# Doubling keys and queries into the other 64 partitions: a DMA in place of a GpSimd copy

## The chip, the cores and the metric

The kernel runs on one core of a Trainium2 chip. The metric is device time in microseconds from one launch; times stand as the median of the timed runs. The engines are TensorE (matrix products), VectorE, ScalarE, GpSimd and SyncE (SP in the profile), which issues DMAs; the DMAs themselves run on 16 DMA engines.

## The reference

One inference step of a two-layer encoder for 512 prompt frames and 32 sample frames (the sample has a past of 1024 frames). Each layer projects the normed input, runs three kinds of attention, gates and merges them, and then runs a feed-forward layer with a short convolution. The three kinds are stick-breaking attention (SB, 8 heads of 64), differential attention (DF, 4 heads with two maps of 64) and latent attention (ML, 8 heads). Cut to what the change touches:

```python
def sb_block(q, q_pos, k, v, k_pos):
    z = jnp.einsum('bqhd,bkhd->bhqk', q, k).astype(jnp.float32) * SB_SCALE
    ...
def diff_block(q, q_pos, k, v, k_pos, lam):
    s = jnp.einsum('bqhmd,bkhmd->bhmqk', q, k).astype(jnp.float32) * DIFF_SCALE
    ...
dq = rmsnorm(z_dq.reshape(B, S, DIFF_HEADS, 2, DIFF_DIM), w['diff_qn_g'])
```

All of it is in float32. The kernel gets this accuracy out of TensorE's rounded format by writing each operand as a high part (rounded) and a low part (the rest).

## The kernel before

The activations lie transposed: 128 features on the partitions, 544 frames (32 sample, 512 prompt) along them. A layer has twelve attention units of 128 features: SB 0 to 3, DF 0 to 3, ML 0 to 3. For an SB or DF unit, `qkv_tasks` (L731) projects keys, then values, then queries, each with 48 matmuls of 272 columns (8 slices, 3 products of parts, 2 halves); between them come projections of gates, which fill TensorE.

A score contracts over 64 features only, half of the partitions. So that one matmul can take high and low part at once, one operand is stacked (`to_stack`, L653: tile u, high parts in one half of the partitions and low parts in the other) and the other doubled (`to_dbl`, L676: tile kk, each head's high and low part present in both halves). SB doubles the keys and stacks the queries; DF doubles the queries and stacks the keys. `to_dbl` therefore runs 16 times: four SB key tiles and four DF query tiles in each of two layers. For each head h, `copy` (ScalarE) writes the rounded high part of 64x512, `tt` (VectorE) the low part of 64x512, and `rnd(..., "pool")` (GpSimd, `pscale`) copies both, 64x1024, into the other half of the partitions. Then the 32 sample frames are split into kn, a part of the same tile. There are two buffers of kk.

The readers are `sb_chain` (L1012) and `df_score` (L1228), which need the doubled tile under the name "k" or "q", and `sb_sample` (L902) and `df_sample` (L1137), which need kn under "kn" or "qn".

The order of the instructions on every engine is not written by hand. `Sched` (L114) simulates the kernel while it is built: every chain of work is a generator (a fiber) with a time at which it is next ready, the one that is ready first is stepped, and each operation adds its estimated duration to its engine (`op`, L127) and 125 ns to the fiber. `put` (L188) files a result with the time at which it is due, `need` (L191) holds a reader until then. The engines then run the resulting lists strictly in order, with semaphores.

All weights come in through SP's queue: `loader` (L214) issues 512 KB loads into four buffers ws, in order of the plan, each when a buffer comes free; the splits into parts (ScalarE, then VectorE, tile wx) free them. Stores of results and the loads of the DF distance tables (alp, als) go through the same queue.

Of the kernel before, what the change touches and what calls it, by code (L numbers as in the profile page):

```python
# [9 lines left out]
F32 = mybir.dt.float32  # L10
# [300 lines left out]
class Kern:  # L311
# [364 lines left out]
    def to_dbl(self, dst, name, z):  # L676


        t = yield from self.al(self.A, [128, 2176], "kk", F32R)
        kk = t[:, :2048].rearrange("p (h s c) -> p h s c", h=2, s=2)  # L680
        kn = t[:, 2048:2112].rearrange("p (s c) -> p s c", s=2)
        rs = (slice(0, 64), slice(64, 128))
        for h, r in enumerate(rs):
            self.copy(kk[r, h, 0], z[r, TS:])
            yield
            self.tt(kk[r, h, 1], z[r, TS:], kk[r, h, 0].bitcast(F32), ALU.subtract)
            yield
            self.rnd(kk[rs[1 - h], h], kk[r, h].bitcast(F32), "pool")
            yield
        yield from self.split(kn, z[:, :TS])  # L690
        self.s.put(dst, name, kk)
        self.s.put(dst, name + "n", kn)

    def zeroed(self, shape, tag):
        t = yield from self.al(self.A, shape, tag, F32R)
# [1807 lines left out]
```

## Time and profile before

| | us |
|---|---|
| median of 3 timed runs | 2085.48 (2082.34 to 2085.56) |
| the profiled execution's own time | 2083.75 |
| its span, first to last instruction | 2082.1 |
| TensorE busy | 2030.7 (98%) |
| VectorE busy | 1614.9 (78%) |
| ScalarE busy | 1310.2 (63%) |
| GpSimd busy | 492.2 (24%) |

In the rows below, PE is TensorE, DVE VectorE, ACT ScalarE, POOL GpSimd and SPq the queue of SyncE. A group of instructions is written as line, engine, operation, tile written <- tiles read, shape. "<-" inside brackets or at the end of a row names what ended the engine's wait. Buffer numbers are left out of the names, so kk stands for both buffers.

### The profile page before, as it was taken

How to read it: one execution, taken by the hardware profiler on the slowest of the kernel's cores; microseconds unless marked ns; L12 is line 12 of the kernel's file. 1: busy time of each engine (PE TensorE's matmuls, PEld its weight loads, DVE VectorE, ACT ScalarE, POOL GpSimd, SP SyncE). 2: the span in 40 equal slices, each digit the busy share in tenths (PEclk: the TensorE clock that was granted, in tenths of full speed). 3: DMA queues.
4: the chain of work that ended last, by engine and by line, in shares of the span. 5: the costliest groups of instructions: out<-in, count | busy, mean ns of one | idle time of the engine just before them, and what ended most of it. 6: DMA issues, size and time to landing. Idle time of an engine off the chain costs nothing.

```text
span 2082.1 us, 42033 instructions
## 1 busy us (share of the span) xinstructions
PE 2030.7 (98%) x15926; PEld 1984.5 (95%) x15926; DVE 1614.9 (78%) x3419; ACT 1310.2 (63%) x2889; POOL 492.2 (24%) x810
## 2 busy tenths in 40 slices
PE   7999999999999999999999999999999999999999
PEld 7999999988999999999989999999889999999999
DVE  7897887888685996598568878887886869955973
ACT  6887676877554564366468777667775555644651
POOL 1344322334200221032023343313342002210310
PEclk9999999999999999999999999999999999999999
DMA  5333433421663232332433334333216622323332
GB/s 205 103 104 125 137 125 107 129 73 48 207 200 111 73 101 84 110 99 86 130 121 104 104 125 149 120 107 112 80 41 219 206 93 91 92 83 102 102 90 87
DMA packets 86218, 238.45 MB, mean 115 GB/s; under 512 B 10304, under 2 KB 11200, under 8 KB 86016
## 3 DMA queue, kind: packets, MB, share of 16 engines
q1 hardware_dynamic: 82240, 223.51, 33.7%
q0 software_dynamic: 3776, 12.26, 1.7%
q8 instruction: 125, 2.05, 0.4%
q14 instruction: 77, 0.63, 0.1%
HBM read 201.52 MB, written 34.21 MB: 113 GB/s over the span
## 4 chain that ended last, share of the span: by engine, by line
PE 77%; DVE 12%; ACT 4%; issue 4%; DMA 1%; POOL 1%; SPq 0%; POOLq 0%; ACTq 0%; DVEq 0%
PE z L410 41%; PE g L410 26%; PE pv L410 8%; DVE wx L347 2%; PE z L416 2%; DVE tf L347 1%; DVE w L347 1%; ACT w L340 1%; ACT p L340 1%; DVE tr L347 1%; DMA ws<-wts 1%; ACT wx L340 1%; DVE pk L347 1%; DVE kk L347 1%; DVE sgl L355 1%
## 5 line engine op out<-in xcount | busy, mean ns | idle before, releaser
L410 PE MATMUL g<-h,wx 128*128 128x272 f32 x5208 | 761.1, 292 | 9.2 <-ACT wx L340 9.0
L410 PEld LDWEIGHTS g<-h,wx 128*128 128x128 f32 x5208 | 696.7, 189 | 17.4 <-ACT wx L340 9.0
L410 PE MATMUL z<-act,wx 128*128 128x272 f32 x4632 | 586.7, 288 | 5.6 <-DVE wx L347 5.6
L410 PEld LDWEIGHTS z<-act,wx 128*128 128x128 f32 x4632 | 581.6, 189 | 6.7 <-DVE wx L347 6.7
L340 ACT ACTIVATE wx<-ws 128x512 fp32r<-128x512 f32 (+2 forms) x554 | 306.9, 555 | 392.9 <-PE z L410 256.3
L347 DVE TENSOR_TENSOR wx<-ws,wx 128x512 fp32r<-128x512 f32 (+2 forms) x554 | 338.6, 612 | 205.9 <-ACT wx L340 202.1
L410 PE MATMUL z<-h,wx 128*128 128x272 f32 x1368 | 179.0, 289 | 0.0
L410 PEld LDWEIGHTS z<-h,wx 128*128 128x128 f32 x1368 | 174.8, 190 | 0.0
L340 ACT ACTIVATE w<-z 128x256 f32<-128x256 f32 (+9 forms) x212 | 91.6, 441 | 44.9 <-PE pv L410 26.2
L347 DVE TENSOR_TENSOR tf<-g,rstd 128x272 f32<-128x272 f32 x184 | 80.0, 435 | 39.8 <-PE g L410 34.7
L2054 POOL COPY conv<-ap 128x2 f32<-128x2 f32 x34 | 21.1, 622 | 317.2 <-DVE ap L347 317.2
L1917 POOL COPY conv<-ap 128x2 f32<-128x2 f32 x10 | 18.2, 1816 | 300.0 <-DVE ap L347 300.0
L410 PE MATMUL pv<-w,vst 128*128 128x512 f32 (+3 forms) x352 | 81.8, 322 | 3.2 <-DVE w L347 1.8
L2041 POOL COPY ap<-gp 128x2 f32<-128x2 f32 x34 | 63.8, 1876 | 81.0 <-ACT wx L340 59.7
L340 ACT ACTIVATE wy<-ws 128x512 fp32r<-128x512 f32 x68 | 42.9, 631 | 60.2 <-PE z L410 34.9
L368 POOL TENSOR_SCALAR tr<-tf 128x544 fp32r<-128x544 f32 (+2 forms) x66 | 45.8, 693 | 141.1 <-ACT tf L340 97.7
L355 DVE SCALAR_TENSOR_TENSOR cc<-ap,gp,cc 128x546 f32<-128x546 f32 x88 | 68.8, 782 | 4.0 <-ACT cc L340 3.8
L340 ACT ACTIVATE p<-p 128x512 f32<-128x512 f32 (+4 forms) x160 | 70.2, 463 | 1.1
L340 ACT ACTIVATE wx<-sgl 128x512 fp32r<-128x512 f32 x102 | 63.4, 627 | 11.1 <-PE z L410 7.1
L347 DVE TENSOR_TENSOR wx<-sgl,wx 128x512 fp32r<-128x512 f32 x102 | 67.7, 685 | 2.3 <-ACT wx L340 2.2
L368 POOL TENSOR_SCALAR kk<-kk 64x1024 fp32r<-64x1024 f32 x32 | 40.6, 1268 | 119.8 <-DVE kk L347 108.4
L347 DVE TENSOR_TENSOR w<-z,w 128x512 fp32r<-128x512 f32 (+5 forms) x124 | 55.9, 466 | 16.3 <-ACT w L340 16.1
(273 smaller groups left out, 3676.4 us busy)
## 6 DMA issues: line engine op xcount, KB each, us to landing
ws<-wts SPq DMA_DIRECT2D x246, 512.0 KB, 3.6
ws<-wts SPq DMA_DIRECT2D x56, 256.0 KB, 3.0
ws<-wts SPq DMA_DIRECT2D x36, 384.0 KB, 3.0
sgl<-sig SPq DMA_DIRECT2D x46, 272.0 KB, 3.2
ws<-wts SPq DMA_DIRECT2D x32, 320.0 KB, 3.0
sig<-tf SPq DMA_DIRECT2D x36, 272.0 KB, 2.1
tf<-od POOLq DMA_DIRECT2D x24, 272.0 KB, 4.7
od<-oa SPq DMA_DIRECT2D x16, 272.0 KB, 2.5
```

Of the source, the lines that this page charges most:

```text
L340: self.nc.scalar.activation(out=out, in_=in_, func=func, **kw)
L347: self.nc.vector.tensor_tensor(out=out, in0=in0, in1=in1, op=op)
L355: self.nc.vector.scalar_tensor_tensor(out=out, in0=in0, scalar=scalar, in1=in1, op0=op0, op1=op1)
L368: self.nc.gpsimd.tensor_scalar(out=out, in0=in_, scalar1=s1, scalar2=1.0, op0=ALU.mult, op1=ALU.mult)
L410: self.nc.tensor.matmul(out=out, lhsT=lhsT, rhs=rhs, start=start, stop=stop, skip_group_check=not chk)
L416: self.nc.tensor.transpose(out, in_, self.ident[:p, :p])
L1917: nc.gpsimd.tensor_copy(out=cv[:, 0:2], in_=ap[:, 546:548])
L2041: nc.gpsimd.tensor_copy(out=ap[:, 0:2], in_=self.gain(G_ST + 2 * i, 2))
L2054: nc.gpsimd.tensor_copy(out=cv[:, 0:2], in_=ap[:, 546:548])
```

## The change

In `to_dbl`, the two GpSimd copies of a tile become two DMAs on SP's queue. The planner is told nothing of an engine for them; instead the doubled tile is due 2500 ns after the second DMA is issued, and kn is filed first, with its own time.

```diff
-            self.rnd(kk[rs[1 - h], h], kk[r, h].bitcast(F32), "pool")
+            self.nc.sync.dma_start(out=kk[rs[1 - h], h].bitcast(F32), in_=kk[r, h].bitcast(F32))
+            late = self.s.cur.ready + 2500.0
             yield
         yield from self.split(kn, z[:, :TS])
+        self.s.put(dst, name + "n", kn)
+        self.s.cur.ready = max(self.s.cur.ready, late)
         self.s.put(dst, name, kk)
-        self.s.put(dst, name + "n", kn)
```

## Rows read from the trace of the kernel before

**Rows 1.** The page's totals: busy us, share of the span, instructions.
```profile
PE 2030.7 (98%) x15926; PEld 1984.5 (95%) x15926; DVE 1614.9 (78%) x3419; ACT 1310.2 (63%) x2889; POOL 492.2 (24%) x810
```
**Rows 2.** Windows by stage: window, its length, busy us of PE, PEld, DVE, ACT, POOL.
```profile
40.00:370.00 330.00, 327.41 (x2583) 315.12 (x2582) 272.65 (x640) 244.94 (x584) 112.34 (x212) 1.00 0.36 120
370.00:545.00 175.00, 165.88 (x1246) 157.16 (x1245) 141.60 (x315) 127.31 (x321) 62.46 (x89) 0.99 0.27 84
1080.00:1405.00 325.00, 321.92 (x2541) 309.46 (x2540) 265.89 (x627) 238.98 (x566) 109.86 (x209) 1.00 0.35 116
1405.00:1580.00 175.00, 165.71 (x1232) 156.81 (x1231) 140.29 (x312) 125.66 (x318) 61.80 (x89) 0.98 0.26 84
```
**Rows 3.** Waits of PE: who ended them, us in total, times, longest us.
```profile
PE z L416 <- POOL p L368: 2.6, 7, 0.6
...
PE z L410 <- DVE w L347: 2.2, 2, 1.1
```
**Rows 4.** Tile kk's own view: ns of one, least, median and most; first and last start.
```profile
L347 DVE TENSOR_TENSOR kk<-tf,kk x48: 171/676/1012, 31.5 to 1370.0; 64x512 fp32r<-64x512 f32 x32, 128x32 fp32r<-128x32 f32 x16
```
**Rows 5.** Groups by shape: busy us, mean ns of one, idle before.
```profile
L368 POOL TENSOR_SCALAR kk<-kk 64x1024 fp32r<-64x1024 f32 x32 | 40.6, 1268 | 119.8 <-DVE kk L347 108.4 <-DVE w L347 11.0
...
L347 DVE TENSOR_TENSOR tr<-tf,tr 128x544 fp32r<-128x544 f32 x46 | 33.0, 718 | 4.9 <-POOL tr L368 4.5
...
L347 DVE TENSOR_TENSOR w<-w,w 128x544 fp32r<-128x544 f32 x8 | 7.1, 883 | 0.0
```
**Rows 6.** Timeline of unit DF1 in layer 0: start us, us, engine, line, operation.
```profile
254.51 1.71 SPq L219 DMA_DIRECT2D ws<-wts  x3
...
255.73 1.01 DVE L347 TENSOR_TENSOR kk<-tf,kk 64x512 fp32r<-64x512 f32 x1
...
256.89 1.04 POOL L368 TENSOR_SCALAR kk<-kk 64x1024 fp32r<-64x1024 f32 x1 [0.69 <-DVE kk L347]
...
257.13 1.38 DVE L347 TENSOR_TENSOR w<-w,w 128x544 fp32r<-128x544 f32 x1
...
258.57 0.51 PE L410 MATMUL z<-w,cr 128*128 128x512 f32 x2 [1.09 <-DVE w L347]
...
260.14 0.56 PE L410 MATMUL z<-u,kk 128*128 128x128 f32 x4
```
**Rows 7.** DMA issues: queue, count, KB each, median us from issue to landing.
```profile
dk<-tf SPq DMA_DIRECT2D x8, 272.0 KB, 2.1
...
b<-als SPq DMA_DIRECT2D x8, 264.0 KB, 5.0
b<-alp SPq DMA_DIRECT2D x8, 256.0 KB, 4.2
```
**Rows 8.** Timelines of SB0, DF0, DF2, DF3, layer 0: second subtraction, first reader.
```profile
37.05 0.69 DVE L347 TENSOR_TENSOR kk<-tf,kk 64x512 fp32r<-64x512 f32 x1
...
40.88 1.51 PE L410 MATMUL z<-u,kk 128*128 128x128 f32 x8
...
218.95 0.81 DVE L347 TENSOR_TENSOR kk<-tf,kk 64x512 fp32r<-64x512 f32 x1
...
224.20 0.97 PE L410 MATMUL z<-u,kk 128*128 128x128 f32 x7
...
292.71 0.69 DVE L347 TENSOR_TENSOR kk<-tf,kk 64x512 fp32r<-64x512 f32 x1
...
295.66 1.08 PE L410 MATMUL z<-u,kk 128*128 128x128 f32 x8
...
329.75 0.69 DVE L347 TENSOR_TENSOR kk<-tf,kk 64x512 fp32r<-64x512 f32 x1
...
334.45 0.73 PE L410 MATMUL z<-u,kk 128*128 128x128 f32 x5
```
**Rows 9.** Timeline of ScalarE: a wait for a weight load in layer 0.
```profile
231.68 0.63 ACT L340 ACTIVATE wx<-ws 128x512 fp32r<-128x512 f32 x1 [2.01 <-DMA ws<-wts]
```
**Rows 10.** Windows, columns as in rows 2: 225 to 245 us.
```profile
225.00:245.00 20.00, 19.89 (x148) 18.61 (x147) 18.37 (x58) 14.03 (x36) 7.34 (x11) 1.00 0.50 162
```

## The prediction

> **What bounds the kernel now.** I read the page's totals first. TensorE is busy 98% of the span, GpSimd 24% [rows 1]: the engine from which work is taken is far from being the bound, and the engine that is the bound keeps all its instructions. A gain can therefore only come out of TensorE's idle time. Second I read the windows by stage, because a share over the whole span says nothing of the stage that is edited. The doubling belongs to the stick-breaking and differential units, which run in 40 to 370 us (layer 0) and 1080 to 1405 us (layer 1). There TensorE is idle 330.00 - 327.41 = 2.59 us and 325.00 - 321.92 = 3.08 us, together 5.67 us; the latent-attention stages behind them, which double nothing with this helper, are idle 9.12 and 9.29 us, 18.41 us in all [rows 2]. So if the edit removed every wait in its own stages it would win 5.67 us, 0.27% of the time. Third come the waits of TensorE: GpSimd ends only 2.6 us of them, and these are on the probability tile p, not on kk; two waits of 1.1 us each end with VectorE on the tile w [rows 3]. No row there names kk.
>
> **What the edit removes.** 32 GpSimd copies of 64x1024, mean 1268 ns: two for each of 16 doubled tiles (eight SB key tiles, eight DF query tiles), 40.6 us of GpSimd [rows 5]. GpSimd is not late for TensorE on kk, so those 40.6 us as such are worth nothing. What they cost is what they do to VectorE. The subtraction that makes the low half of kk takes 676 ns in the median and 1012 ns at most [rows 4]; the subtraction on w of 128x544 takes 883 ns in the mean, where the same shape on tr takes 718 [rows 5]. The timeline of unit DF1 shows why that matters: VectorE's kk subtraction of 1.01 us, then a GpSimd copy of kk at 256.89, and across it the w subtraction, 1.38 us from 257.13; TensorE then waits 1.09 us for exactly that w [rows 6]. Without the copies the two subtractions should take about 0.68 and 0.72, so VectorE gives back 0.33 + 0.66 = 1.0 us ahead of that wait. The wait occurs twice, once in each layer, 2.2 us in total [rows 3]. I book **-2.2 us** (bounds: 0, if another subtraction is late next; -5.7, if all idle time of the two stages went).
>
> [...]
>
> **What the edit adds on the DMA side.** 32 transfers of 64 partitions x 4096 bytes, 256 KB, from SBUF to SBUF on SP's queue, 8.4 MB beside the 238 MB that are moved already. The trace has no SBUF-to-SBUF transfer and none between partition halves. Nearest rows, issue to landing: 2.1 us for the store dk<-tf of 272 KB from 128 partitions; 4.2 us for the 256 KB load alp; 5.0 us for the 264 KB load als, the only large one on 64 partitions, which always goes out right behind alp [rows 7]. So 2.1 is the end below, with a free queue, and 5.0 the end above, behind other traffic. I take 2.1 where no weight load was issued within the microsecond ahead, and 4.2 where the transfer falls into a train of them.
>
> [...]
>
> What hides the transfer is the room between the end of a tile's second subtraction and the first matmul that reads the tile. For the SB keys it is wide: keys are projected first, and the V and Q projections stand between, 96 matmuls at 330/2583 = 128 ns [rows 2], over 12 us; only the first unit of layer 0 is tight, 37.74 to 40.88 = 3.1 us [rows 8], still above 2.1. For the DF queries, which are projected last, the room is 224.20 - 219.76 = 4.44 us (DF0), 260.14 - 256.74 = 3.40 (DF1) [rows 6, 8], 295.66 - 293.40 = 2.26 (DF2) and 334.45 - 330.44 = 4.01 (DF3) [rows 8]; layer 1 repeats them to within a few tenths. Set against these: DF0 2.1 in 4.44, nothing; DF1 falls behind the train of three weight loads that SP issues from 254.51 on [rows 6], 4.2 - 3.40 = 0.8 us; DF2 2.1 in 2.26, which the issue and the semaphores use up, 0.3 us; DF3 2.1 in 4.01, nothing. TensorE takes its instructions in order, so such a wait is paid in full. 1.1 us a layer, **+2.2 us** (bounds: 0, and with 5.0 everywhere the 11.8 us of the rival below).
>
> **SP's queue.** The transfer waits on SP for VectorE's subtraction, and behind it stand weight loads, the loads of past keys and values, alp and als, and the stores. At some 0.33 us an issue SP's own time is 32 x 0.33 = 10.6 us of a mostly waiting engine. The cover is the lead of the weights. The trace has a natural test: ScalarE sat idle 2.01 us, up to 231.68, until a weight load landed, and TensorE was nevertheless busy 19.89 of the 20.00 us from 225 to 245 [rows 9, 10]. Some two microseconds of delay on this queue thus cost nothing. If that cover were gone, each microsecond would be paid once for each of the 16 tiles. I book 0.
>
> **The planner.** The order of all engines is written out by a simulation (Sched), and the edit changes its inputs. Before, kk was due after the second subtraction plus copy, plus both parts of kn: 125 + 1254 + 125 + 122 + 125 + 108 + 125 = 1984 ns by the kernel's own formulas. After it is due 125 + 2500 = 2625 ns behind that subtraction, but the subtraction itself comes 1254 + 125 = 1379 ns earlier, as the first half's copy no longer stands ahead of it: 2625 - 1984 - 1379 = 738 ns earlier in all. The small tile kn, which the sample path reads, is due about 2.8 us earlier, as both copies are gone ahead of it. Both move order in the edited stages. The TensorE idle of the two layers is 9.12 and 9.29 us in the stage behind, although the layers come in differently [rows 2], so the plan falls back into the same order after a disturbance, and I book 0 with a few microseconds either way.
>
> **Sum.** -2.2 + 2.2 + 0 + 0 = 0. The profiled execution took 2083.75 us (2082.1 of span and 1.65 around it), 1.73 below the median 2085.48 of the three timed runs. The four executions average 2084.3, and that is the forecast: no change.
>
> **Rivals.**
> 1. *The transfers are late for TensorE* (slower). Price: each of the eight DF tiles takes 5.0 us. Then 0.56 + 1.60 + 2.74 + 0.99 = 5.9 us a layer, 11.8 in all, less 2.2 gained: 2084.3 + 9.6 = 2093.9 us. It decides from a landing of about 2.3 us on in DF2 and 3.4 us in DF1. For it: the als row, the weight train at 254.51, and that the planner allows only 2.5 us. Against it: stores on a free queue land in 2.1 us, and three of the four units leave 3.4 us or more. Chance 0.25.
> 2. *VectorE's relief shortens more than the two w waits* (faster), and the earlier kn lets the units end earlier, so that the latent stage meets more gate projections to fill its 18.4 us of idle. Price: the 5.7 us of the edited stages gone, or a third of the 18.4 with the w waits: 2084.3 - 5.7 = 2078.6, or 2084.3 - 6.1 - 2.2 = 2076.0. For it: VectorE is the second busiest engine, 272.65 of 330 us [rows 2]. Against it: TensorE is already 99.2% busy there, and the idle latent stage waits for chains in which kk has no part. Chance 0.18.
> 3. *It does not matter at all*: transfers hidden, the w wait taken over by the next late subtraction; also about 2084. It is within the forecast's band.
>
> **How the numbers follow.** A change of 0.2%, 4.2 us, is about what a measurement of this kernel can tell from none. The forecast and rival 3 hold 0.57, with a band of their own of 2081 to 2088. Rival 1 beyond 4.2 us holds 0.25, rival 2 beyond 4.2 us 0.18. The range reaches most of the way to both: 2078.5 below (rival 2 by the edited stages alone), 2092 above (three quarters of rival 1).
>
> **What would show it.** In the profile after: GpSimd near 492 - 41 = 452 us; a row kk<-kk among the DMA issues, 32 of 256 KB, its landing time the judge between forecast (2 to 3 us) and rival 1 (4 to 5); the waits of TensorE with or without a row that ends in that DMA; the 1.1 us waits on w gone and the VectorE mean on w near 720 ns; the idle time of the windows 40 to 370 and 1080 to 1405 near 2.5 us each. The forecast is wrong if TensorE waits over 6 us for kk transfers, or if idle time outside the two stages moves by more than 4 us.

## The result, and the profile after

| | before | after |
|---|---|---|
| median of 5 runs each, us | 2082.66 (2081.20 to 2085.56) | 2094.67 (2091.87 to 2097.63) |
| ratio after / before, 95% interval | | 1.0052 [1.0041, 1.0062] |
| span of the profiled execution, us | 2082.1 | 2092.9 |
| TensorE idle: span less busy, us | 51.4 | 58.5 |

The runs before are the three timed ones and two more. The changed kernel is 0.52% slower, about 12 us. The forecast of no change was wrong, and the time lies above its range.

The totals of the page after (busy us, share of the span, instructions), to be read beside [rows 1]:

```profile
PE 2034.4 (97%) x15926; PEld 1987.6 (95%) x15926; DVE 1608.4 (77%) x3419; ACT 1305.9 (62%) x2889; POOL 450.8 (22%) x778
```

The edit did what it says: GpSimd lost 32 instructions and 41.4 us. The same TensorE instructions now take 3.7 us more of busy time and have 7.1 us more of idle time between them: 10.8, the difference of the two spans.

The windows by stage after (the columns of [rows 2]: window, length, busy us of PE, PEld, DVE, ACT, POOL, granted clock, DMA share, GB/s). The edges are moved with the stages. The five short windows belong to the paragraph on the clock below:

```profile
40.00:377.00 337.00, 331.30 (x2590) 317.66 (x2590) 270.92 (x640) 244.21 (x587) 91.72 (x198) 0.99 0.41 128
377.00:552.00 175.00, 165.93 (x1249) 157.47 (x1248) 140.76 (x314) 126.39 (x320) 64.26 (x89) 0.99 0.26 85
1088.00:1415.00 327.00, 320.45 (x2512) 308.91 (x2512) 261.19 (x621) 234.96 (x562) 88.56 (x193) 0.99 0.39 124
1415.00:1590.00 175.00, 165.19 (x1246) 155.86 (x1245) 141.46 (x314) 126.54 (x319) 64.01 (x89) 1.00 0.27 86
296.00:300.00 4.00, 2.00 (x14) 1.70 (x14) 2.24 (x8) 1.57 (x4) 0.64 (x1) 0.94 0.79 242
300.00:305.00 5.00, 5.00 (x31) 5.00 (x31) 3.32 (x12) 2.94 (x10) 0.56 (x2) 0.70 0.28 79
...
1295.00:1300.00 5.00, 1.43 (x13) 1.32 (x11) 2.94 (x7) 1.80 (x4) 1.07 (x2) 0.97 1.00 274
1300.00:1305.00 5.00, 5.00 (x30) 5.00 (x31) 2.03 (x8) 1.57 (x5) 0.00 (x0) 0.69 0.23 91
...
1340.00:1345.00 5.00, 5.00 (x30) 5.00 (x30) 3.44 (x13) 2.51 (x10) 0.03 (x1) 0.66 0.36 121
```

The time came in where the edit is. TensorE idles 337.00 - 331.30 = 5.70 us in the edited stage of layer 0 and 6.55 in that of layer 1, where [rows 2] had 2.59 and 3.08. The latent-attention stages idle 9.07 and 9.81, as in [rows 2] (9.12 and 9.29).

The waits of TensorE after (who ended them, us in total, times, longest), beside [rows 3]:

```profile
PE z L410 <- DMA kk<-kk: 11.3, 11, 3.6
...
PE z L416 <- POOL p L368: 2.6, 7, 0.6
...
PE z L410 <- DVE w L347: 0.5, 1, 0.5
```

A new row heads the list. Eleven waits, 11.3 us, end with the new transfers; the two waits of 1.1 us on w are gone, as forecast, and one of 0.5 us stands at another place. The row of the transfers among the DMA issues after (queue, count, KB each, median us from issue to landing):

```profile
kk<-kk SPq DMA_DIRECT2D x32, 256.0 KB, 4.0
```

The planner allows them 2.5 us and the forecast took 2.1 for most. They take 4.0 in the median, and from 2.8 to 5.8.

The timeline of two units after, DF2 in layer 0 and DF1 in layer 1 (start us, us, engine, line, operation; in brackets the wait ahead of it and who ended it):

```profile
291.60 1.39 DVE L347 TENSOR_TENSOR kk<-tf,kk 64x512 fp32r<-64x512 f32 x2
291.61 0.33 SPq L219 DMA_DIRECT2D ws<-wts  x1
292.33 1.15 SPq L688 DMA_DIRECT2D kk<-kk  x2
...
297.95 0.41 PE L410 MATMUL z<-u,kk 128*128 128x128 f32 x2 [1.59 <-DMA kk<-kk]
...
298.76 0.94 PE L410 MATMUL z<-u,kk 128*128 128x128 f32 x6 [0.41 <-DMA kk<-kk]
...
1292.49 0.47 SPq L688 DMA_DIRECT2D kk<-kk  x1
1293.06 0.52 SPq L219 DMA_DIRECT2D ws<-wts  x1
...
1293.93 0.47 SPq L688 DMA_DIRECT2D kk<-kk  x1
...
1299.88 1.41 PE L410 MATMUL z<-u,kk 128*128 128x128 f32 x5 [3.57 <-DMA kk<-kk]
```

In DF2 both subtractions now run back to back, both transfers go out together 0.7 us behind a 512 KB weight load (ws), and they land 5.5 and 5.6 us after their issue. In DF1 of layer 1 a weight load comes between the two: the first transfer lands in 2.9 us and the second in 5.8, and TensorE waits 3.57 us, the longest of the eleven. Read so over all 32 transfers, the ten that go out less than a microsecond behind a weight load land in 4.1 to 5.8 us, the eight that go out while no weight load is in flight in 2.8 to 3.8, and the fourteen with an earlier load still in flight in 2.9 to 5.6.

**The clock behind the waits.** After the waits of DF2 the granted clock from 300 to 305 us is 0.70, and TensorE gets through 31 matmuls; behind the 3.57 us wait it is 0.69, and behind DF2 of layer 1, which waited 1.53 and 0.32 us at 1338 to 1340, it is 0.66. Part of each stretch ran at 0.50: read by single microseconds, the granted clock is 0.50, 0.50, 0.52, 1.00 and 1.00 from 300 on, 0.50, 0.50, 0.50, 0.96 and 1.00 from 1300 on, and 0.81, 0.50, 0.50, 0.50 and 0.98 from 1340 on. Before, the stretch of 300 to 305 us held 36 matmuls at 1.00, and no 5 us stretch of the two edited stages lay below 0.90. By the granted clock the three stretches lost 5 x (0.30 + 0.31 + 0.34) = 4.75 us, an estimate; TensorE's busy time rose by 3.7.

A fall of the clock does not follow every such wait. The kernel with due 5500 (below) was profiled twice. At about 700 us, outside the edited stages, TensorE waits 1.97 us in one profile and 2.00 in the other; the 5 us that follow, in this order:

```profile
700.70:705.70 5.00, 5.00 (x30) 5.00 (x29) 5.00 (x12) 3.34 (x5) 2.74 (x1) 0.67 0.34 108
...
698.70:703.70 5.00, 5.00 (x40) 5.00 (x41) 5.00 (x11) 3.03 (x5) 2.25 (x1) 1.00 0.36 108
```

Their busy times differ by 4.0 us (2030.6 and 2026.6), so the 3.7 of one pair of profiles measures little. Over the timed runs the mean granted clock is 0.993 in the changed kernel (five runs, 0.992 to 0.994) and 0.996 in the kernel before (the 23 runs beside the first four experiments, 0.994 to 0.998): 0.003 of 2090 us, some 6 us, an estimate. But the kernel with only the queries by DMA (below), which is as slow, has 0.996 as well. What the clock cost the change as a whole stays open.

### The profile page after: what moved, and what is told of

It reads as the page before. It is cut to its first block, busy times and chain, and to the rows that moved or that the text cites. A ratio compares the mean times of both kernels' runs of the same rounds, so it can differ in the third digit from the quotient of the medians.

```text
span 2092.9 us, 42063 instructions
## 1 busy us (share of the span) xinstructions
PE 2034.4 (97%) x15926; PEld 1987.6 (95%) x15926; DVE 1608.4 (77%) x3419; ACT 1305.9 (62%) x2889; POOL 450.8 (22%) x778
## 4 chain that ended last, share of the span: by engine, by line
PE 78%; DVE 11%; ACT 4%; issue 4%; DMA 2%; POOL 1%; SPq 0%; ACTq 0%; POOLq 0%; DVEq 0%
PE z L410 41%; PE g L410 27%; PE pv L410 8%; PE z L416 2%; DVE wx L347 2%; DMA kk<-kk 2%; DVE tf L347 1%; ACT p L340 1%; ACT w L340 1%; ACT wx L340 1%; DVE kk L347 1%; DVE tr L347 1%; DVE nm L372 1%; ACT tf L340 1%; DVE sgl L355 1%
## 5 line engine op out<-in xcount | busy, mean ns | idle before, releaser
L368 POOL TENSOR_SCALAR tr<-tf 128x544 fp32r<-128x544 f32 (+2 forms) x66 | 50.3, 762 | 160.0 <-ACT tf L340 117.7
L410 PE MATMUL z<-u,kk 128*128 128x384 f32 (+3 forms) x256 | 54.2, 328 | 11.5 <-DMA kk<-kk 11.3
```

The lines of the kernel that those rows point to most:

```text
L368: self.nc.gpsimd.tensor_scalar(out=out, in0=in_, scalar1=s1, scalar2=1.0, op0=ALU.mult, op1=ALU.mult)
L410: self.nc.tensor.matmul(out=out, lhsT=lhsT, rhs=rhs, start=start, stop=stop, skip_group_check=not chk)
```

## The experiments

Theory A: the time is lost because the transfers of the DF query tiles land later than the first reader asks for them. Its rivals: the new plan (kn filed first, another due time) costs the time by itself; or the transfers are fast, and it is SP's queue, where they stand behind weight loads, that makes them late. "Stage" below is the time from the first z<-u,kk matmul of a layer to its first z<-kk,u matmul, both layers added: the SB and DF units and the projections that the plan puts between them and behind them. (The number of its matmuls differs by a dozen from plan to plan, some 1.5 us at 128 ns each; kernels with the same plan have the same number.) It is 731.8 us before and 740.2 after. The kernel that ran twice (5500, below) gives 724.7 and 724.1, which shows how well it repeats.

**Keys by DMA, queries by GpSimd.**

```diff
-            self.nc.sync.dma_start(out=kk[rs[1 - h], h].bitcast(F32), in_=kk[r, h].bitcast(F32))
-            late = self.s.cur.ready + 2500.0
+            late = 0.0
+            if name == "k":
+                self.nc.sync.dma_start(out=kk[rs[1 - h], h].bitcast(F32), in_=kk[r, h].bitcast(F32))
+                late = self.s.cur.ready + 2500.0
+            else:
+                self.rnd(kk[rs[1 - h], h], kk[r, h].bitcast(F32), "pool")
```

> The DMA for the 8 SB key tiles alone; the 8 DF query tiles are copied by GpSimd as before. Theory A: no wait of TensorE for kk transfers, as V and Q projections stand between; 2081 to 2085 us. Theory B: in between, about 2088. Theory C: half of the loss, about 2088.

Measured 2079.30 us, ratio 0.9980 [0.9972, 0.9989]: faster than before, and below the range of each theory. No wait of TensorE ends with a transfer. The keys' transfers are hidden, and taking GpSimd off the SB units, with the plan that goes with it, is worth some 4 us.

**Queries by DMA, keys by GpSimd.** The same edit with `if name == "q"`.

> The DMA for the 8 DF query tiles alone; the 8 SB key tiles are copied by GpSimd as before. Theory A: the full loss, about 11 us of waits for kk transfers, 2092 to 2096 us. Theory C: half of the loss, about 2088.

Measured 2094.59 us, ratio 1.0053 [1.0041, 1.0066], the whole of the loss. The wait of TensorE in its profile:

```profile
PE z L410 <- DMA kk<-kk: 9.1, 13, 1.4
```

The loss hangs on the eight DF query tiles, as theory A has it. Its waits are 2.2 us fewer than after and its time is the same, so it probably lacks what the keys' half brings.

**The new plan with the old copies.** The GpSimd copy stands where the DMA stood, and the planner is told nothing of it; the order of TensorE's instructions is that of the changed kernel.

```diff
-            self.nc.sync.dma_start(out=kk[rs[1 - h], h].bitcast(F32), in_=kk[r, h].bitcast(F32))
+            self.nc.gpsimd.tensor_scalar(out=kk[rs[1 - h], h], in0=kk[r, h].bitcast(F32), scalar1=1.0, scalar2=1.0,
+                                         op0=ALU.mult, op1=ALU.mult)
```

> The planner is told exactly what it is told in the changed kernel (no GpSimd time, due 2500 ns later, kn filed first), but the copies still run on GpSimd. Theory A: no loss, 2081 to 2085 us, as the copy is done 1.1 to 1.3 us after the subtraction, inside 2.5. Theory B: the loss is there without a single transfer, about 2093 us.

Measured 2085.45 us, ratio 1.0006 [0.9997, 1.0015]. The plan by itself costs nothing that can be told, so that rival falls. It also parts the order from the copies in the waits on w. With the copies still there the w subtraction of 128x544 takes 714 ns in the mean, where [rows 5] had 883: the new order moved it from under the copy, and the two waits in DF1 are gone. But two others, of 0.83 and 1.31 us, have come among the SB units of layer 1, and the sum is nearly that of [rows 3]:

```profile
PE z L410 <- DVE w L347: 2.1, 2, 1.3
```

In the same order without the copies, the changed kernel has 0.5 us of such waits. So the order moved the waits on w, and the copies' absence took 1.6 us of them away.

**The transfer with a later due time.** The only edit is that the planner takes 5.5 us for a transfer.

```diff
-            late = self.s.cur.ready + 2500.0
+            late = self.s.cur.ready + 5500.0
```

> Same transfers as the changed kernel; only the time at which the planner takes a doubled tile to be due goes from 2500 to 5500 ns after the issue. Theory A (TensorE waits because the query tiles land 4.4 to 5.8 us after their issue while the readers are ordered for 2.5): the 11.3 us of waits for kk transfers fall under 2 us, the time comes back to 2081 to 2085 us. Theory B (the new order costs by itself): another order again, no forecast, nearer 2095. Theory C (the 8.4 MB of added traffic and the issues on SP's queue cost): unchanged, 2093 to 2096.

Measured 2077.39 us, ratio 0.9969 [0.9958, 0.9981]: faster than both kernels, and below the range of theory A. Its totals (busy us, share, instructions):

```profile
PE 2030.6 (98%) x15926; PEld 1986.3 (96%) x15926; DVE 1609.3 (77%) x3419; ACT 1308.5 (63%) x2889; POOL 448.1 (22%) x778
```

Its waits of TensorE on w and kk (us in total, times, longest):

```profile
PE z L410 <- DVE w L347: 0.9, 2, 0.4
PE z L410 <- DMA kk<-kk: 0.4, 1, 0.4
```

Its timeline of DF2 in layer 0:

```profile
288.22 0.33 SPq L219 DMA_DIRECT2D ws<-wts  x1
...
291.65 1.60 SPq L688 DMA_DIRECT2D kk<-kk  x2
...
298.35 1.09 PE L410 MATMUL z<-u,kk 128*128 128x128 f32 x8
```

The same bytes go through the same queue in as many transfers; what is gone is the wait, 11.3 to 0.4 us. The reader of DF2 comes 6.7 us behind the first issue without a bracket. The plan also moved: the weight load now goes out 3.4 us ahead of the transfers, and both land in 3.0 us. TensorE's busy time is 2030.6 us, as in [rows 1].

> The kernel with the transfers and due 5500 once more, on the same chip as the two others, since 0.3% is to be compared. 2076 to 2081 us.

The repeat measured 2078.43 us, ratio 0.9975 [0.9965, 0.9984]. Its one wait on a transfer is 1.0 us, at the same place (DF1 of layer 0) as the 0.4 us above: that transfer landed 6.7 us after its issue, where it took 5.8 in the first profile.

**Between and beyond.** `late` with 4000 and with 7000.

> The changed kernel with a due time of 4000 ns in place of 2500 (5500 gave 2077.4 us). Theory A by doses: the DF tiles that land 4.4 to 5.8 us after their issue stay 0.4 to 1.8 us late, the earlier ones are covered; 2 to 5 us of waits for kk transfers, 2078 to 2084 us. If the time does not lie between those at 2500 and 5500, the due time is not what sets it.

Measured 2086.64 us, ratio 1.0016 [1.0007, 1.0025]; TensorE waits 3.7 us for transfers, five times. It lies between, as theory A has it, but slower than expected: from 2500 to 4000 the waits fall by 7.6 us and the time by 8.0; from 4000 to 5500 the waits fall by 3.3 us and the time by 8 to 9. The later step holds some 5 us that are not transfer waits; what they are stays open.

> The changed kernel with due 7000 ns. Theory A: no wait for kk transfers is left (0.4 us at 5500), so no further gain from them; 2076 to 2081 us. If later readers keep helping by themselves, below 2075; if the units now end late for their oldest buffers, above 2081.

Measured 2081.65 us, ratio 0.9998 [0.9989, 1.0006]. The waits on transfers stay gone and the stage is down to 722.7 us, but waits come in behind it, in the latent-attention stage of layer 1: those on p are 4.0 us in all (2.6 before), the longest now 1.4 at 1466 us, and 2.0 us, at 1439 and 1510 us, end with VectorE on kk, which there is the tile of latent attention. A later reader costs more than it saves from here on.

**The other queue.** `nc.gpsimd.dma_start` in place of `nc.sync.dma_start`, all else as changed.

> The changed kernel with the 32 transfers issued on GpSimd's queue instead of SP's, due 2500 as in the change. If the transfers are late because they stand behind a weight load in SP's own queue, they land nearer 3 us and most of the 11.3 us of waits goes: 2080 to 2086 us. If they are late because all DMAs share the same engines and the halves are slow, landing stays at 4 to 5 us or grows (the trace of before has 4.7 us for a 272 KB load on this queue) and the time stays at 2093 to 2098 us.

Measured 2094.73 us, ratio 1.0044 [1.0030, 1.0057]. Its wait of TensorE for the transfers:

```profile
PE z L410 <- DMA kk<-kk: 9.1, 12, 1.7
```

Its row among the DMA issues (median landing last):

```profile
kk<-kk POOLq DMA_DIRECT2D x32, 256.0 KB, 3.9
```

Off SP's queue the landing is 3.9 us against 4.0 and the loss nearly the whole: the rival of SP's queue falls as the main cause. On SP's queue one transfer, the second of DF1 in layer 1, did go out some 0.7 us after its subtraction had ended, behind the issue of a weight load; here it does not, and the longest wait shrinks from 3.6 to 1.7 us.

**The landing by itself.** The kernel before with 24 groups of transfers added behind its end, where nothing else runs; its own time is therefore not comparable. `lo` and `up` are the two halves of the partitions, `c` 1024 columns, `fence` makes a group wait for the one before, `load` is a 512 KB weight load.

```diff
+        for r in range(3):
+            fence()
+            nc.sync.dma_start(out=A[up, c], in_=A[lo, c])
...
+        for r in range(3):
+            fence()
+            nc.sync.dma_start(out=B[:, 0:512], in_=A[:, 0:512])
...
+        for r in range(3):
+            fence()
+            load(r)
+            nc.sync.dma_start(out=A[up, c], in_=A[lo, c])
+        for r in range(3):
+            fence()
+            load(r)
+            nc.sync.dma_start(out=A[up, c], in_=A[lo, c])
+            nc.sync.dma_start(out=B[lo, c], in_=B[up, c])
...
```

> The kernel before, followed by 24 groups of transfers on an otherwise quiet core; only their landing times are read, the time is longer by the added tail. Half to other half, 256 KB: 2.8 us (the least in the changed kernel). Half onto the same half, 256 KB: 2.8 to 3.2 if reaching only half of the partitions is what slows it. 128 partitions, 256 KB within SBUF: 2.1 to 2.4. 128 partitions, 256 KB store: 2.1. Two opposite halves at once: 3 to 4.2 each. One half behind a 512 KB weight load: 4.4 to 4.6. Both halves behind a weight load: 5.0 to 5.6. The same two on GpSimd's queue: sooner than 5 if the order within SP's queue is the cause, not sooner if it is the shared engines.

The lines of four of these transfers (duration of the issue in ns, then us from issue to landing): half to half, 128 partitions, half to half behind a weight load, and the second of two behind a load:

```profile
L2264 SPq DMA_DIRECT2D pr<-pr x3: 461/478/492, 2084.9 to 2092.0; - x3
...
DMA to landing us min/median/max: 2.8/2.9/2.9
...
L2270 SPq DMA_DIRECT2D pr<-pr x3: 465/475/486, 2106.3 to 2112.1; - x3
...
DMA to landing us min/median/max: 2.3/2.3/2.3
...
L2281 SPq DMA_DIRECT2D pr<-pr x3: 461/467/467, 2137.3 to 2149.6; - x3
...
DMA to landing us min/median/max: 4.6/5.3/5.4
...
L2286 SPq DMA_DIRECT2D pr<-pr x3: 587/588/596, 2156.6 to 2171.9; - x3
...
DMA to landing us min/median/max: 5.9/6.2/6.2
```

Alone and on idle engines the transfer takes 2.9 us, from one half onto the same half as well; 2.1 is never reached, and a 256 KB store from 128 partitions takes 2.0. One weight load ahead makes it 5.3, and the pair as DF2 sends it 5.7 and 6.2 (5.8 and 6.4 with the pair on GpSimd's queue), more than expected in each case. Both conditions are in the changed kernel: 2.8 us is its least landing, with no load in flight, and DF2's are 5.5 and 5.6. For this kernel the probe names a condition, a load in flight, and the three groups of landings above agree with it. That the landings in the kernel have this cause is argued from there; an experiment that took the loads away was not made. The same bytes within SBUF on 128 partitions land in 2.3 us; why 64 partitions take 0.6 us longer was not shown.

**What the missing copies are worth.** The same plan as the due time of 5500, with GpSimd copies in place of the transfers: the edit of the new plan with the old copies, with 5500. TensorE's instructions stand in the same order in both, so the difference lies in the copies and the transfers, not in that order.

> GpSimd copies, no transfer, and the planner told what it is told in the kernel with due 5500. That kernel is 6 us faster than before. If the gain is the new order's (readers put later, so that TensorE meets them ready), it is here too: 2076 to 2081 us. If it is GpSimd's and VectorE's relief, it is not: 2083 to 2087 us, as with the copies and due 2500.

Measured 2087.36 us, ratio 1.0020 [1.0011, 1.0029], at the upper end of the second range. Its totals:

```profile
PE 2034.0 (97%) x15926; PEld 1987.6 (95%) x15926; DVE 1626.9 (78%) x3419; ACT 1308.9 (63%) x2889; POOL 489.9 (23%) x810
```

Its waits of TensorE on w:

```profile
PE z L410 <- DVE w L347: 4.8, 5, 1.3
```

The copies among its groups by shape (busy us, mean ns of one | idle before):

```profile
L688 POOL TENSOR_SCALAR kk<-kk 64x1024 fp32r<-64x1024 f32 x32 | 38.2, 1193 | 104.6 <-DVE kk L347 95.0 <-DVE w L347 8.8
```

Against the transfers with 5500, VectorE is busy 17.6 us longer with the same 3419 instructions, TensorE waits 4.8 us for w where it waited 0.9, and the stage takes 731.2 us where it took 724.7; 6.1 of these 6.5 us are idle time of TensorE. Four kernels, ratio to before:

| due time told to the planner | GpSimd copies | transfers |
|---|---|---|
| 2500 | 1.0006 | 1.0052 |
| 5500 | 1.0020 | 0.9969, 0.9975 |

The gain lies in neither of the two alone: with due 5500 the missing copies are worth 6.5 us of the stage, and the kernel keeps such a gain only where the readers come late enough for the transfer (or the room hides it, as for the keys).

**GpSimd kept busy, reading nothing.** Is it GpSimd's time or its reading that slows VectorE? The kernel with transfers and 5500, and ahead of each transfer two GpSimd memsets of its destination, 64x1024.

```diff
+            for _ in range(2):
+                self.nc.gpsimd.memset(kk[rs[1 - h], h].bitcast(F32), 0.0)
```

> The kernel with the transfers and due 5500 (2077.4 and 2078.4 us), with two GpSimd memsets of 64x1024 into the half that the transfer then overwrites: GpSimd is given about as much time back as the copies took, but reads nothing. If the copies cost by slowing VectorE while they read (VectorE busy 1626.9 us with copies, 1609.3 with transfers, in the same order of instructions), VectorE stays near 1609 and the time at 2077 to 2081 us. If they cost because other GpSimd work stands behind them, the time goes back to 2084 to 2088 us.

Measured 2080.99 us, ratio 0.9986 [0.9977, 0.9995]. Its totals:

```profile
PE 2030.5 (98%) x15926; PEld 1984.9 (95%) x15926; DVE 1611.7 (77%) x3419; ACT 1309.9 (63%) x2889; POOL 513.0 (25%) x842
```

The memsets among its groups by shape:

```profile
L689 POOL MEMSET kk<- 64x1024 f32 x64 | 60.8, 951 | 3.2
```

60.8 us of GpSimd that only writes add 2.4 us to VectorE (1609.3 to 1611.7); 38.2 us that read and write added 17.6. That speaks for reading. The memsets are not tied to the subtraction as the copies were and start elsewhere, so it is not a clean pair; and the kernel is 2.6 to 3.6 us slower than without them (measured on other chips).

## Why the prediction was wrong, step by step

**What bounds the kernel** held: 7.1 of the 10.8 us are idle time of TensorE, nearly all of it in the edited stages, and the latent stages stayed as they were.

**What the edit removes** was right in kind and too small. GpSimd gave back 41.4 us, forecast 40.6, and they were worth little as such (60.8 us of memsets cost 2.6 to 3.6); their worth lay mostly in VectorE. But I booked only the two w waits that the trace named, 2.2 us. The relief is wider: TensorE's idle time apart from the waits on transfers fell by 11.3 - 7.1 = 4.2 us in the changed kernel, and with due 5500, in the same order of TensorE, the copies cost 6.5 us of the stage. My bound of 5.7, the price of rival 2, was nearer than my value.

**What the edit adds on the DMA side** is the step that failed, in two places. The first is the price: "I take 2.1 where no weight load was issued within the microsecond ahead" rested on the store dk from 128 partitions [rows 7]. Half to half it is 2.8 to 2.9 us at best, and 4.1 to 5.8 within a microsecond of a weight load. The row to lean on was als, 64 partitions right behind another load, 5.0 us [rows 7], which I set as the end above. The second is the traffic: I took the places of the weight loads from the trace before, where one GpSimd copy stood between the two subtractions of a tile. Without it the second transfer follows the first sooner (0.7 us later in DF2 and DF3, 1.3 in DF0), and both go out close behind a load. My paragraph on the planner has the second subtraction 1379 ns earlier, but I did not carry that over to here; and I looked only at the second subtraction, though the trace before has a load 0.8 and 0.6 us ahead of the end of the first in DF0 and DF2. So the units that I booked as free, DF0 and DF3, and DF2 at 0.3 us, paid 1.2, 1.3 and 2.0 us in layer 0 (the waits in the timeline's brackets). DF1, the one for which I expected the train, paid 0.83, which meets the 0.8 of the sum by luck: no load stood ahead of it, its second transfer landed in 3.5 us, and its room was shorter than I had it. 11.3 us stand in the place of my 2.2, and they are over the 6 us that I gave as a sign of being wrong. The rooms are not what failed: DF2's reader would have started at 297.95 - 1.59 = 296.36, 3.4 us behind the end of its second subtraction, where I had 2.26. The four rooms of layer 0, read so, are 3.0, 2.5, 3.4 and 3.9 us where I had 4.44, 3.40, 2.26 and 4.01, and each is above 2.1: had the landing been 2.1, TensorE would not have waited.

**The clock** is a term that my sum did not have. I wrote that a wait "is paid in full"; behind three of the waits the clock fell besides, 4.75 us by the granted clock of these stretches. Whether it belongs in the sum is open: the totals have 3.7 us more of busy time, and two profiles of one kernel differ by 4.0.

**The SB keys, SP's queue and the planner's order**, each booked at 0, held: the keys alone cost no wait, the queue of GpSimd gives nearly the same time, and the new order with the old copies is 1.0006. The keys' rooms were smaller than the "over 12 us" that I worked out: in the trace before, SB3 of layer 1 has 6.3 us (1188.05 to 1194.32), still above the longest landing of 5.8. The planner's 2500 ns, which I named only as an argument for rival 1, is a promise on which the order of the readers is built. It is below the landing, so the plan puts the readers where TensorE must wait; 5500 removes that.

**Rival 1** is what happened, mechanism and place. Its 2093.9 us stands beside 2094.67, in part by luck: its waits of 11.8 were 11.3, but its gain of 2.2 was 4.2, and 3.7 us of busy time, for which it has no term, make up for that (11.3 - 4.2 + 3.7 = 10.8, the difference of the two spans). Rival 2's mechanism, VectorE's relief, is true at the same time, covered by the other: with the readers moved, 2077.39 and 2078.43 us stand beside its 2078.6. That number too is met in part by luck. TensorE's idle time in the stage fell by 3.6 and 2.9 us in the two profiles, not by 5.7; the rest is shorter busy time, which the profiles do not explain.

## What to carry to other kernels

A transfer that replaces a copy is to be priced with the traffic that will be in flight when it goes out (here 2.9 us alone, 5.3 behind one load), from the row that has the same partitions and the same company, not from a lone store (2.1); and the plan must be told that price, or the readers are put where they wait. Work taken from an engine that is far from the bound can still be worth time through the engine it disturbs (here 6.5 us of the stage, from an engine busy 24%); look for the same instruction with the same shape at different durations. And of the five places read here where a busy TensorE waited 1.9 to 3.6 us, four had a granted clock of 0.66 to 0.70 in the 5 us that follow and one had 1.00; this belongs in the range of a forecast.

## What the runs showed of the hardware that was not expected

- An SBUF-to-SBUF transfer of 256 KB from one half of the partitions to the other lands 2.9 us after its issue on idle engines, as does one onto the same half; with the same bytes on 128 partitions it is 2.3 us. Behind one 512 KB load it takes 5.3 us; a pair behind a load 5.7 and 6.2.
- Two such transfers in opposite directions, the second issued 0.5 us behind the first, land in 3.1 and 3.7 us, each from its own issue: the pair is done 4.3 us after its first issue, where one alone takes 2.9.
- In the changed kernel the three stretches of 5 us behind waits of 2.0, 3.6 and 1.9 us in a unit had a granted clock of 0.70, 0.69 and 0.66 and 30 or 31 matmuls; before, one of them had 36 at 1.00. The same wait of 2.0 us in two profiles of one kernel was followed by 0.67 in one and 1.00 in the other.
- 38.2 us of GpSimd copies cost VectorE 17.6 us of busy time and the kernel 9 us (2087.36 against 2078.43, the same order of TensorE's instructions). The instructions of TensorE, the bound engine, are the same.
